# Stick-breaking attention: two heads scored in the two halves of TensorE's rows, triangular sums from two parts of the softplus

## The chip, the cores and the metric

One NeuronCore of a Trainium2 chip runs the whole program. The metric is device time in microseconds (us) from launch to end; lower is better. Three runs of the kernel before gave 775.49, 776.06 and 776.16 us, so its time is their median, 776.06 us.

## What is computed

Two transformer layers over 256 tokens of width 1024. Layer 0 mixes with stick-breaking attention (8 heads of 64) beside an S5 state-space model, layer 1 with a sparse attention; each mixer is followed by a layer norm, a mixture of 16 experts and another layer norm. The change touches the stick-breaking attention of layer 0 alone:

```python
def stick_breaking_attention(q, k, v):      # heads of 64, scale = 1/8
    for i in range(L // Q_BLOCK):           # 2 blocks of 128 queries
        z = einsum('bqhd,bkhd->bhqk', q[:, q0:kend], k[:, :kend]) * scale
        mask = s[None, :] < t[:, None]
        log_1mb = where(mask, -softplus(z), 0.0)
        after = cumsum(log_1mb, axis=3, reverse=True) - log_1mb
        w = where(mask, exp(log_sigmoid(z) + after), 0.0)
        outs.append(einsum('bhqk,bkhd->bqhd', w, v[:, :kend]))
```

With z - softplus(z) for log_sigmoid(z), the exponent is z minus the sum of the softplus from the key itself to the last allowed key.

## The kernel before

Keys lie on the partitions and queries in the free dimension, so a head's scores are one PSUM tile `z` of 384 used columns: 256 for the first 128 keys against all queries, 128 for the second 128 keys against the second 128 queries. `stick` (line 1210) returns three steps, which `mixer0` (line 1067) calls by hand as S, W and O:

- `scores(h)`, lines 1215 to 1230: two float32 matmuls with 64 rows of contraction (L1219 with 256 columns, L1220 with 128), whose operands lie in partitions 0 to 63 for even heads and 64 to 127 for odd ones; then two bfloat16 matmuls (L1222) that add -1e30 where the mask forbids. Then softplus(z) = max(z, 0) + ln(1 + exp(-|z|)): three ScalarE activations of 128x384 (L1225, L1227, L1228) and one VectorE operation (L1229), into a tile `sp` of the pool `b2` (9 slots).
- `weights(h)`, lines 1232 to 1240: three float32 matmuls with 128x128 triangles of -1 (L1234, one with 256 columns and two with 128) subtract the running sums inside PSUM; ScalarE takes the exponential (L1239).
- `values(hp)`, lines 1242 to 1252: for a pair of heads, four float32 matmuls (L1250), each head in one half of the output's partitions, and the split of the result into two float32r parts (L1251, L1252).

A float32 matmul stands in the trace as two instructions (two passes), a float32r one as one.

PSUM has two pools of four banks, `acc` and `mm`. Each `z` holds an `acc` bank from its scores until its exponential (L1239). After the heads the same four `acc` banks become `out`, the sums of the output projection: first the residual (L259, 32 instructions in this mixer), then jobs of float32r matmuls in three terms (L203 to L205 in `mm3`).

Between the heads' steps stand other steps of the mixer: `kq(j)` (L985, 32 instructions each for the keys and the queries of a pair of heads, copied out by ScalarE at L1128 and L1131), the S5 kernel (L868), the transposes of `s5_transpose` (L895 on TensorE, eight copies of 128x512 by ScalarE at L896), `s5_inputs` (L905, which needs all of these copies), the S5 states on VectorE (L920 to L931) and `s5_output` (L957 on TensorE, which needs the states), its GELU (L1060 to L1065), transposes (L973), and the gated unit behind them.

Weights come by DMA in tiles of 1 MB in the pool `u` (20 slots of 8 KB a partition), which holds the mixer's large work tiles as well. `issue` (line 131) orders further tiles as long as fewer than a cap are ahead; SyncE issues them in order and waits where the slot given to a tile is not free yet.

The order of the calls in `mixer0` is written by hand and serves as priority; a scheduler then fixes the order on each engine when the program is built, and lets a later step ahead where an earlier one isn't ready. Only in the mixture of experts is TensorE's order exactly as written.

Of the kernel before, what the change touches and what calls it, by code (L numbers as in the profile page):

```python
# [10 lines left out]
F32 = mybir.dt.float32  # L11
# [8 lines left out]
P = 128  # L20
D = 1024
KC = D // P
T = 256
# [28 lines left out]
class K:  # L52
# [47 lines left out]
    def mm(self, shape=(P, 512), dt=F32):  # L100
        return self.psp.tile(list(shape), dt, tag="mm", bufs=4, name=self.uid("mm"))
# [965 lines left out]
    def mixer0(self):  # L1067
# [79 lines left out]
        kq = lambda j: (cols(k_out(j)), cols(q_out(j)))  # L1147
        kq(0), kq(1)
        self.s5_toeplitz(self.s5_kernel(ca, vx[:, 1].rearrange("p (a r n) -> p a r n", a=16, r=2)), kts)
        S(0), S(1)  # L1150
        kq(2)
        S(2), S(3)
        kq(3)
        W(0), S(4)
        self.s5_transpose(bbp[0], w1t[0])
        W(1), S(5)
        self.s5_transpose(bbp[1], w1t[1])
        O(0), W(2)
        self.stage(10)
        ps = self.s5_inputs(U, w1t)  # L1160
        self.issue(CAP[1])
        states = self.s5_states(ps, X, bbp[1].rearrange("p a d h -> p (a d h)").rearrange("p (j n) -> p j n", j=4))
        ys = self.s5_output(U, X, kts, ca, w1t[0].rearrange("p a n -> p (a n)"))
        n = lambda g: next(g, None)
        n(states), W(3), O(1), S(6), n(states), W(4), n(states), S(7), n(states), W(5), O(2), n(states), W(6), n(states)
        W(7), O(3)
        self.table("sigmoid_and_others")
        n(ys), n(ys)
# [41 lines left out]
    def stick(self, qT, kT, V, oa):  # L1210

        nc = self.nc
        st = {}

        def scores(h):
            s = slice((h % 2) * 64, (h % 2) * 64 + 64)
            z = self.acc()
            k, q = kT[s, h // 2], qT[s, h // 2]
            nc.tensor.matmul(z[:, 0:T], k[:, 0:P], q, start=True, stop=False, skip_group_check=True)  # L1219
            nc.tensor.matmul(z[:, T:T + P], k[:, P:T], q[:, P:T], start=False, stop=False, skip_group_check=True)  # L1220
            for c in (0, T):
                nc.tensor.matmul(z[:, c:c + P], self.identb, self.negb, start=False, stop=False, skip_group_check=True)  # L1222

            sp = self.b2((P, 384))
            a = nc.scalar.activation(sp, z[:, 0:384], AF.Abs)  # L1225
            self.follow(a, self.logs)
            nc.scalar.activation(sp, sp, AF.Exp, scale=-1.0)  # L1227
            nc.scalar.activation(sp, sp, AF.Ln, bias=1.0)  # L1228
            nc.vector.scalar_tensor_tensor(sp, z[:, 0:384], 0.0, sp, ALU.max, ALU.add)  # L1229
            st[h] = (z, sp)  # L1230

        def weights(h):
            z, sp = st[h]
            mm = lambda o, l, r, stop: nc.tensor.matmul(z[:, o[0]:o[1]], l, r, start=False, stop=stop, skip_group_check=True)  # L1234
            mm((0, T), self.ntri[:, 0], sp[:, 0:T], False)
            mm((P, T), self.ntri[:, 1], sp[:, T:T + P], True)
            mm((T, T + P), self.ntri[:, 0], sp[:, T:T + P], True)
            w = self.b2((P, 384))
            nc.scalar.activation(w, z[:, 0:384], AF.Exp)  # L1239
            st[h] = w  # L1240

        def values(hp):
            o = self.mm()
            for kb in range(2):
                for c in range(2):
                    h = hp * 2 + c
                    w = st[h]
                    r = w[:, 0:T] if kb == 0 else w[:, T:T + P]
                    d = o[c * 64:c * 64 + 64, 0:T] if kb == 0 else o[c * 64:c * 64 + 64, P:T]
                    nc.tensor.matmul(d, V[:, kb, h * 64:h * 64 + 64], r, start=(kb == 0), stop=(kb == 1), skip_group_check=True)  # L1250
            nc.scalar.activation(oa[:, 0, hp], o[:, 0:T], AF.Copy)  # L1251
            nc.vector.tensor_tensor(oa[:, 1, hp], o[:, 0:T], oa[:, 0, hp].bitcast(F32), ALU.subtract)  # L1252

        return scores, weights, values


# [479 lines left out]
```

## Time and profile before

| what | value |
|---|---|
| median of three runs | 776.06 us |
| the profiled execution's own time | 776.09 us |
| its span, first to last instruction | 774.4 us |
| TensorE matmul busy | 752.6 us (97%) |
| VectorE, ScalarE, GpSimd busy | 326.3, 207.4, 46.8 us |
| bytes moved by DMA | 241.00 MB, mean 311 GB/s |

The span is the time between the first and the last instruction in the trace; 1.7 us of the execution's time lie outside it. Busy times of matmuls overlap, since a matmul's record lasts from its start to the modelled arrival of its last result. What a matmul costs in a dense stretch is the distance from its start to the start of the next.

### The profile page before, as it was taken

To read this page: it belongs to the slowest core of one execution; us is meant where nothing else is said; L and a number is where in the kernel's file an instruction comes from. 1 tells how busy PE (TensorE), PEld (TensorE's weight loads), DVE (VectorE), ACT (ScalarE), POOL (GpSimd) and SP (SyncE) were. 2 spreads that over 40 slices of the span, in tenths; PEclk is the share of its full clock that TensorE was granted. 3 is DMA by queue.
4 is the path that set the end of the run, shared out by engine and by line. 5 is a ranking of instruction groups with operands and counts; after the bars stand their busy time and mean duration, and the time that the engine had idled before them with its cause. 6 is when DMAs were issued, how large, how long until landed. Compare 5 with 4: busy or idle time off the path is not lost. (4 is left out here: it accounts for less than half of the span.)

```text
span 774.4 us, 10523 instructions
## 1 busy us (share of the span) xinstructions
PE 752.6 (97%) x4115; PEld 415.4 (54%) x4115; DVE 326.3 (42%) x836; ACT 207.4 (27%) x421; POOL 46.8 (6%) x45
## 2 busy tenths in 40 slices
PE   9999999999999999999899999999999999999993
PEld 7588778643434334333878666687434334343332
DVE  9992647611212112114956799836212112211123
ACT  1344435211101101001625577632121001011002
POOL 1010000002000000001020142300002000000000
PEclk9999999999999999999999999999999999999998
DMA  8839879889999999999975100397799999999921
GB/s 320 312 110 183 312 281 409 289 308 381 348 423 421 421 422 421 421 417 421 421 251 209 55 1 0 149 386 281 261 368 372 401 421 421 421 421 421 419 90 59
DMA packets 42540, 241.00 MB, mean 311 GB/s; under 512 B 8145, under 2 KB 9681, under 8 KB 15569
## 3 DMA queue, kind: packets, MB, share of 16 engines
q1 hardware_dynamic: 42480, 240.23, 79.8%
q8 instruction: 34, 0.56, 0.3%
q14 instruction: 26, 0.20, 0.1%
HBM read 238.38 MB, written 1.84 MB: 310 GB/s over the span
## 5 line engine op out<-in xcount | busy, mean ns | idle before, releaser
L493 PE MATMUL mm<-u,s 128*64 128x512 f32 x960 | 219.4, 598 | 0.0
L493 PEld LDWEIGHTS mm<-u,s 128*64 128x64 f32 x960 | 63.9, 136 | 120.3 <-issue 107.7
L523 PE MATMUL mm<-u,b 128*64 128x512 f32 x512 | 113.1, 593 | 0.0
L528 ACT ACTIVATE b<-mm,gslot 128x512 fp32r<-128x512 f32 x32 | 22.0, 688 | 256.1 <-PE mm L523 253.2
L529 DVE SCALAR_TENSOR_TENSOR b<-mm,gslot,b 128x512 fp32r<-128x512 f32 x32 | 24.0, 750 | 146.9 <-ACT b L528 146.9
L523 PEld LDWEIGHTS mm<-u,b 128*64 128x64 f32 x512 | 36.4, 137 | 71.9 <-issue 70.2
L195 DVE TENSOR_TENSOR s<-u,s 128x1024 fp32r<-128x1024 f32 x37 | 45.5, 1235 | 28.4 <-ACT s L192 28.3
L576 DVE TENSOR_TENSOR b<-b,mm 128x256 f32<-128x256 f32 x32 | 12.0, 418 | 106.9 <-PE mm L493 106.8
L192 ACT ACTIVATE s<-u 128x1024 fp32r<-128x1024 f32 x37 | 38.7, 1056 | 42.0 <-PE acc L205 29.0
L985 PE MATMUL mm<-u,u 128*128 128x256 f32 x208 | 48.0, 392 | 0.6 <-DMA u<-w_in 0.6
L985 PEld LDWEIGHTS mm<-u,u 128*128 128x128 f32 x208 | 40.7, 197 | 7.4 <-issue 1.7
L354 ACT ACTIVATE s<-mm,c_k_all 128x256 f32<-128x256 f32 x32 | 18.1, 565 | 96.7 <-PE mm L469 96.7
L469 PE MATMUL mm<-b,u 128*128 128x256 f32 x160 | 39.0, 325 | 0.0
L203 PE MATMUL acc<-s,u 128*128 128x512 f32 x96 | 38.0, 396 | 0.5 <-ACT u L1205 0.5
L534 PE MATMUL acc<-b,b 128*128 128x512 f32 x128 | 38.4, 421 | 0.1
L205 PE MATMUL acc<-s,u 128*128 128x512 f32 x96 | 37.8, 394 | 0.0
L204 PE MATMUL acc<-s,u 128*128 128x512 f32 x96 | 37.5, 391 | 0.0
L534 PEld LDWEIGHTS acc<-b,b 128*128 128x128 f32 x128 | 21.4, 188 | 28.4 <-issue 22.7
L469 PEld LDWEIGHTS mm<-b,u 128*128 128x128 f32 x160 | 30.0, 190 | 6.3 <-issue 4.9
L588 DVE COPY b<-mm 128x512 f32<-128x512 f32 x16 | 11.1, 692 | 45.2 <-PE mm L587 45.2
L356 DVE TENSOR_SCALAR s<-mm,c_k_all 128x256 f32<-128x256 f32 x32 | 16.8, 542 | 24.1 <-PE mm L469 23.8
L469 PE MATMUL mm<-b,s 128*128 128x256 f32 x96 | 23.5, 285 | 0.0
(309 smaller groups left out, 1002.2 us busy)
## 6 DMA issues: line engine op xcount, KB each, us to landing
u<-moe SPq DMA_DIRECT2D x180, 1024.0 KB, 11.9
u<-w_in SPq DMA_DIRECT2D x26, 1024.0 KB, 15.0
u<-w_in SPq DMA_DIRECT2D x10, 512.0 KB, 6.9
s<-moe SPq DMA_DIRECT2D x4, 1024.0 KB, 5.8
b<-moe SPq DMA_DIRECT2D x16, 256.0 KB, 8.3
u<-moe SPq DMA_DIRECT2D x8, 512.0 KB, 16.8
u<-xT SPq DMA_DIRECT2D x4, 256.0 KB, 5.7
out<-u SPq DMA_DIRECT2D x4, 256.0 KB, 4.3
```

What stands on the lines that cost most here:

```text
L192: a = self.nc.scalar.activation(s[:, 0], x, AF.Copy)
L195: self.mark = self.nc.vector.tensor_tensor(s[:, 1], x, s[:, 0].bitcast(F32), ALU.subtract)
L203: mm(o, l[0], r[0], start=first, stop=False, skip_group_check=True)
L204: mm(o, l[0], r[1], start=False, stop=False, skip_group_check=True)
L205: self.tail = mm(o, l[1], r[0], start=False, stop=last, skip_group_check=True)
L469: nc.tensor.matmul(pg[:, 0:T], x[:, t, k * P:(k + 1) * P], g.bitcast(F32) if m == 1 else g, start=(i == 0), stop=(i == 2 * m - 1))
L493: self.mark = nc.tensor.matmul(h[c * 64:(c + 1) * 64], xe[:, k, e + c], w[c], start=(k == 0), stop=(k == KC - 1))
L523: self.mark = nc.tensor.matmul(y[c * 64:(c + 1) * 64], hx[:, f, c * 64:(c + 1) * 64], w[:, c * 512:c * 512 + 512], start=(f == 0), stop=(f ...
L528: nc.scalar.activation(yh, y, AF.Copy, scale=gs)
L529: nc.vector.scalar_tensor_tensor(yl, y, gs, yh.bitcast(F32), ALU.mult, ALU.subtract)
L534: self.tail = nc.tensor.matmul(out[half][t], sT[:, t * P:(t + 1) * P], yy, start=False, stop=(p == 7 and j == 1), skip_group_check=True)
L985: self.mark = self.nc.tensor.matmul(ps, w[:, k * P:k * P + P], xT[:, k], start=(k == 0), stop=(k == KC - 1))
```

## The change

`scores` now takes a pair of heads. It takes two `acc` banks, issues the float32 matmuls of the two heads in turn (256 columns of the one, 256 of the other, 128 of the one, 128 of the other; one head's operands lie in partitions 0 to 63, the other's in 64 to 127), and then all four bfloat16 mask matmuls. The softplus of each head is copied by ScalarE to a float32r part, and VectorE computes the rest as a second float32r part; both parts of both heads lie in one new tile of the pool `u`. `weights` multiplies each triangle with both parts: six float32r matmuls (256, 256, 128, 128, 128, 128 columns) instead of three float32 ones. The triangles are copied once to float32r (`tr`). In `mixer0` the calls are placed anew: four calls of `scores` instead of eight, the last of them, for heads 6 and 7, ahead of `s5_inputs` and not among the states; W(1) and W(3) stand earlier as well.

```diff
@@ -1147,22 +1147,22 @@
         kq = lambda j: (cols(k_out(j)), cols(q_out(j)))
         kq(0), kq(1)
         self.s5_toeplitz(self.s5_kernel(ca, vx[:, 1].rearrange("p (a r n) -> p a r n", a=16, r=2)), kts)
-        S(0), S(1)
+        S(0)
         kq(2)
-        S(2), S(3)
+        S(1)
         kq(3)
-        W(0), S(4)
+        W(0), W(1), S(2)
         self.s5_transpose(bbp[0], w1t[0])
-        W(1), S(5)
+        W(2)
         self.s5_transpose(bbp[1], w1t[1])
-        O(0), W(2)
+        O(0), W(3), S(3)
         self.stage(10)
         ps = self.s5_inputs(U, w1t)
         self.issue(CAP[1])
         states = self.s5_states(ps, X, bbp[1].rearrange("p a d h -> p (a d h)").rearrange("p (j n) -> p j n", j=4))
         ys = self.s5_output(U, X, kts, ca, w1t[0].rearrange("p a n -> p (a n)"))
         n = lambda g: next(g, None)
-        n(states), W(3), O(1), S(6), n(states), W(4), n(states), S(7), n(states), W(5), O(2), n(states), W(6), n(states)
+        n(states), O(1), n(states), W(4), n(states), n(states), W(5), O(2), n(states), W(6), n(states)
         W(7), O(3)
         self.table("sigmoid_and_others")
         n(ys), n(ys)
@@ -1211,30 +1211,43 @@
 
         nc = self.nc
         st = {}
-
-        def scores(h):
-            s = slice((h % 2) * 64, (h % 2) * 64 + 64)
-            z = self.acc()
-            k, q = kT[s, h // 2], qT[s, h // 2]
-            nc.tensor.matmul(z[:, 0:T], k[:, 0:P], q, start=True, stop=False, skip_group_check=True)
-            nc.tensor.matmul(z[:, T:T + P], k[:, P:T], q[:, P:T], start=False, stop=False, skip_group_check=True)
-            for c in (0, T):
-                nc.tensor.matmul(z[:, c:c + P], self.identb, self.negb, start=False, stop=False, skip_group_check=True)
-
-            sp = self.b2((P, 384))
-            a = nc.scalar.activation(sp, z[:, 0:384], AF.Abs)
-            self.follow(a, self.logs)
-            nc.scalar.activation(sp, sp, AF.Exp, scale=-1.0)
-            nc.scalar.activation(sp, sp, AF.Ln, bias=1.0)
-            nc.vector.scalar_tensor_tensor(sp, z[:, 0:384], 0.0, sp, ALU.max, ALU.add)
-            st[h] = (z, sp)
+        tr = self.b2((P, 2, P), F32R)
+        nc.scalar.activation(tr, self.ntri, AF.Copy)
+
+        def scores(hp):
+
+            zs = [self.acc() for _ in range(2)]
+            rows = [slice(c * 64, c * 64 + 64) for c in range(2)]
+            for part in range(2):
+                for z, s in zip(zs, rows):
+                    k, q = kT[s, hp], qT[s, hp]
+                    if part == 0:
+                        nc.tensor.matmul(z[:, 0:T], k[:, 0:P], q, start=True, stop=False, skip_group_check=True)
+                    else:
+                        nc.tensor.matmul(z[:, T:T + P], k[:, P:T], q[:, P:T], start=False, stop=False, skip_group_check=True)
+            for z in zs:
+                for c in (0, T):
+                    nc.tensor.matmul(z[:, c:c + P], self.identb, self.negb, start=False, stop=False, skip_group_check=True)
+            parts = self.u([P, 2, 2, 512], F32R)
+            for c, z in enumerate(zs):
+
+                sp = self.b2((P, 384))
+                a = nc.scalar.activation(sp, z[:, 0:384], AF.Abs)
+                self.follow(a, self.logs)
+                nc.scalar.activation(sp, sp, AF.Exp, scale=-1.0)
+                nc.scalar.activation(sp, sp, AF.Ln, bias=1.0)
+                nc.vector.scalar_tensor_tensor(sp, z[:, 0:384], 0.0, sp, ALU.max, ALU.add)
+                hl = parts[:, c]
+                nc.scalar.activation(hl[:, 0, 0:384], sp, AF.Copy)
+                nc.vector.tensor_tensor(hl[:, 1, 0:384], sp, hl[:, 0, 0:384].bitcast(F32), ALU.subtract)
+                st[hp * 2 + c] = (z, hl)
 
         def weights(h):
-            z, sp = st[h]
-            mm = lambda o, l, r, stop: nc.tensor.matmul(z[:, o[0]:o[1]], l, r, start=False, stop=stop, skip_group_check=True)
-            mm((0, T), self.ntri[:, 0], sp[:, 0:T], False)
-            mm((P, T), self.ntri[:, 1], sp[:, T:T + P], True)
-            mm((T, T + P), self.ntri[:, 0], sp[:, T:T + P], True)
+            z, hl = st[h]
+            for o, l, c, n in ((0, 0, 0, T), (P, 1, T, P), (T, 0, T, P)):
+                for j in range(2):
+                    nc.tensor.matmul(z[:, o:o + n], tr[:, l], hl[:, j, c:c + n], start=False, stop=o > 0 and j == 1,
+                                     skip_group_check=True)
             w = self.b2((P, 384))
             nc.scalar.activation(w, z[:, 0:384], AF.Exp)
             st[h] = w
```

## Rows read from the trace of the kernel before

**Rows 1.** The page: TensorE's busy time; TensorE and DMA busy tenths in 40 slices.

```profile
PE 752.6 (97%) x4115; PEld 415.4 (54%) x4115; DVE 326.3 (42%) x836; ACT 207.4 (27%) x421; POOL 46.8 (6%) x45
...
PE   9999999999999999999899999999999999999993
...
DMA  8839879889999999999975100397799999999921
```

**Rows 2.** Stretches of mixer 0: us, busy per engine, granted clock, DMA share, GB/s.

```profile
52.00:70.08 18.08, 18.08 (x93) 15.23 (x89) 9.90 (x11) 8.80 (x18) 2.37 (x2) 1.00 0.70 147
70.08:83.64 13.56, 13.35 (x199) 11.72 (x197) 1.11 (x2) 8.33 (x18) 0.00 (x0) 1.00 1.15 291
83.64:99.36 15.72, 15.72 (x103) 11.74 (x99) 12.54 (x20) 7.58 (x16) 0.00 (x0) 1.00 0.78 276
99.36:118.70 19.34, 19.33 (x248) 13.92 (x248) 10.25 (x15) 7.59 (x11) 0.00 (x0) 1.00 0.76 291
```

**Rows 3.** Timeline, TensorE, scores of heads 0 and 1: start us, length us, instruction.

```profile
51.99 0.70 PE L1219 MATMUL acc<-u 64*128 64x256 f32 x2
52.52 0.38 PE L1220 MATMUL acc<-u 64*128 64x128 f32 x2
52.84 0.28 PE L1222 MATMUL acc<-c_k_bits 128*128 128x128 bf16 x2
...
54.02 0.43 PE L985 MATMUL mm<-u,u 128*128 128x256 f32 x1
```

**Rows 4.** The same timeline: masks, transposes, triangular sums, values.

```profile
72.55 0.29 PE L1222 MATMUL acc<-c_k_bits 128*128 128x128 bf16 x2
72.67 1.37 PE L895 MATMUL mm<-c_k_all,u 128*128 128x128 f32 x11
73.88 1.04 PE L1234 MATMUL acc<-b,b 128*128 128x256 f32 x6
74.75 1.15 PE L895 MATMUL mm<-c_k_all,u 128*128 128x128 f32 x9
...
77.92 0.87 PE L1250 MATMUL mm<-b,u 128*64 128x256 f32 x8
78.72 1.14 PE L1234 MATMUL acc<-b,b 128*128 128x256 f32 x6
```

**Rows 5.** The same timeline: float32r matmuls of 256 columns, then of 160 columns.

```profile
119.93 0.28 PE L203 MATMUL mm<-u,s 128*128 128x256 f32 x1
120.05 0.28 PE L204 MATMUL mm<-u,s 128*128 128x256 f32 x1
...
171.47 0.45 PE L505 MATMUL mm<-R,b 128*128 128x160 f32 x2
171.85 0.65 PE L493 MATMUL mm<-b,s 128*64 128x512 f32 x2
```

**Rows 6.** Groups, weight loads, 52 to 126 us: busy us, mean ns | idle before.

```profile
L203 PEld LDWEIGHTS mm<-u,s 128*128 128x128 f32 x16 | 3.0, 191 | 0.0
...
L1222 PEld LDWEIGHTS <-c_k_bits 128*128 128x128 bf16 x16 | 0.9, 97 | 1.0
```

**Rows 7.** Timeline, TensorE: values of heads 2 and 3 with scores of head 6.

```profile
84.72 0.65 PE L1250 MATMUL mm<-b,u 128*64 128x256 f32 x2
...
87.25 0.43 PE L1234 MATMUL acc<-b,b 128*128 128x256 f32 x1
```

**Rows 8.** Groups of ScalarE, then VectorE, from 52 us on.

```profile
L1227 ACT ACTIVATE b<-b 128x384 f32<-128x384 f32 x8 | 4.2, 521 | 0.1
...
L1229 DVE SCALAR_TENSOR_TENSOR b<-acc,b 128x384 f32<-128x384 f32 x8 | 4.4, 554 | 17.7 <-ACT b L1228 17.7
```

**Rows 9.** First expert layer: issue and landing of its last weights; their first matmul.

```profile
L144 SPq DMA_DIRECT2D u<-moe x1: 328/328/328, 331.9 to 331.9; - x1
...
DMA to landing us min/median/max: 16.2/16.2/16.2
...
360.60 1.94 PE L523 MATMUL mm<-u,b 128*64 128x512 f32 x8
```

## The prediction

> **What bounds the kernel now.** I read the page first: TensorE's matmuls are busy 97% of the span and its row of slices is full from end to end, while DMA drops in several slices [rows 1]. Matmul records overlap, so this says only that the engine seldom stands still; what a matmul costs must come from distances between starts. Then the mixer that is changed, cut into stretches at its landmarks: W(0) at 70.08 us, the end of `s5_inputs` at 83.64, the start of `s5_output` at 99.36, the gated unit at 118.70 [rows 2]. TensorE is filled in all four, VectorE is long only in the third (12.54 of 15.72 us, the S5 states), ScalarE at most 8.33 of 13.56 us. So a microsecond of matmuls saved here should end the mixer a microsecond earlier, unless a chain on another engine comes up behind it.
>
> Last, whether the rest of the program passes the gain on. In the first expert layer DMA is full [rows 1], which could swallow it. The last tile of its weights was issued at 331.9 us, landed 16.2 us later (348.1), and its first matmul began at 360.60 [rows 9]: it lay ready for 12.5 us. The layer is bound by TensorE and can start some 12 us earlier before weights are missing. I carry a gain of 5 us to the end in full.
>
> **Scores.** Heads 0 and 1 run from 51.99 to 54.02 us, 2.03 us [rows 3], between other shapes on both sides. Within a head, L1219 takes 0.53 and L1220 0.32 us: its four passes (two of 256 columns, two of 128) would be 0.65 us at the pace of L1234, which puts 1024 columns through in 0.87 us without a change of shape (73.88 to 74.75 [rows 4]), and the other 0.20 us is what it costs to go from one shape of the array to another (the first weight load isn't hidden, the last result drains). No row of before shows two row halves at work together. The nearest row is L1250: the same eight passes of 256, 256, 128 and 128 columns for two heads, halved in the output's columns and not in the rows: 77.92 to 78.72, 0.80 us [rows 4], so the halves ran side by side. The four mask matmuls behind it cost 0.06 us each (72.55 to 72.67 for two [rows 4]), 0.24 us. New pair: 1.04, and 0.05 for a weight load of 128 columns instead of 64: 1.09 us. Saved 0.94 a pair, four pairs: **3.8 us**. If the halves don't run side by side, only one entry into the shape and one way out of it are saved in each pair, some 0.3 us: 1.2 us in all. I take 3.8, since nothing in the shapes but the direction of the split differs, and keep 1.2 as the end.
>
> The Trainium skill (TensorE: Matmul & The Clock Gate, Part 3: Packing small matmuls) says that packed matmuls start and end strictly in program order; if a float32 matmul's two passes stand together in that order, the second head's first pass could only start with the first head's second. By that rule a pair takes about one pass of 256 columns more, 0.2 us, and the sum below would be 4.2 instead of 5.0 us. The 0.80 us of L1250 leaves no room for such a lag between column halves; for row halves no row shows it.
>
> **Triangular sums.** The three float32 matmuls cost the 0.87 us just read, eight times. The new six are float32r. With 256 columns one costs 0.12 us (119.93 to 120.05 [rows 5]). With 128 columns none is in the trace, so bounds: below, the masks' 0.06 us in bfloat16; in the middle 0.11 us, the pace of the transposes L895, one pass of 128 columns with a weight load each (eleven in 72.67 to 73.88 [rows 4]); above, 0.22 us, if 128 columns in float32r cost as much as the two float32 passes. The pair with 160 columns, 0.38 us with the way in and out of the shape (0.2), is near 0.1 each [rows 5], which excludes little but the upper end. Weight loads decide: a float32r load of 128 columns lasts 191 ns, the bfloat16 one 97 [rows 6], so I expect the load to set the pace, 0.11 us. Head: 2 x 0.12 + 4 x 0.11 = 0.68, saved 0.19, eight heads **1.5 us**. Ends: 2 x 0.12 + 4 x 0.06 = 0.48, saved 3.1; 2 x 0.12 + 4 x 0.22 = 1.12, lost 2.0.
>
> The Trainium skill (the same page, Weight-path perf modes) gives fast weight loads to all types but FP32. If float32r counts as another type, this case goes to its lower end, and the sum would be 6.6 us. The 191 ns speak against it.
>
> **Moved calls.** S(6) ran between the halves of O(1), with a change of shape each time: 84.72 to 87.25, 2.53 us [rows 7], where O(1) by itself costs 0.80 and a head's scores 1.02 (half of 2.03). With S(3) before `s5_inputs` this weaving goes: 0.7 less one entry of 0.2, **0.5 us** (0 to 0.7, as the scheduler may weave something else in).
>
> **Added work beside TensorE.** Eight copies of 128x384 on ScalarE, at about the 0.52 us of L1227 [rows 8]: 4.2 us. Eight subtractions on VectorE at about the 0.55 us of L1229 [rows 8]: 4.4 us. Heads 0 to 3 have their softplus long before W(0), with both engines half idle from 52 to 70 us [rows 2]; the copy of the triangles lies before that. In the second stretch it gets narrow. ScalarE had 8.33 us there. Heads 6 and 7 come in with 3 x 0.52 each, four copies, and W(3)'s exponential: 8.3 + 3.1 + 2.1 + 0.5 = 14.0 us. TensorE's work of that stretch becomes 13.6 + 1.1 (W(3)) + 2.0 (S(3)) less 1.9 (two pairs) and 0.8 (four W): 14.0 us. What is queued behind ScalarE's copies are the copies L896 for which `s5_inputs` waits; but the softplus of heads 6 and 7 can finish behind them. In the third stretch TensorE sinks from 15.7 to about 11 us (W(3), S(6) and S(7) gone, four cheaper W), and VectorE's states, 12.5 less two softplus operations, become as long. The cover is there: the 48 matmuls L203 to L205 of the first output jobs, 512 columns and so twice 0.12 us each [rows 5], can run before `s5_output`. I take **0.8 us** of new waits, between 0 and 3.
>
> **Slots.** Each pair's two parts take a 1 MB slot of `u` until both its W are done, two or three at a time from 55 to 93 us. They come from those of the weights ahead. At the program's mean of 311 GB/s a tile is 3.4 us of DMA, three are 10. SyncE issues in order, so the S5 kernel's own transfers queue behind a weight tile that waits for a slot; `s5_output` at 99.36 us waits for them. DMA has room to catch up before 107 us (shares 0.70 to 0.78 in three of the four stretches [rows 2]), and 12.5 us of cover stand at the far end [rows 9], so I cost this at nothing; without that cover each missing tile costs its 3.4 us.
>
> **Sum.** 3.8 + 1.5 + 0.5 - 0.8 = 5.0 us off the profiled execution's 776.09: 771.1 us. The median of the runs is 776.06, the same within 0.03.
>
> **The rivals.**
> - *The row halves run one after the other, or lag.* Scores save 1.2 instead of 3.8: 773.7 us; with the lag 771.9. For it: no row shows row halves together. Against it: column halves do.
> - *Float32r weights load fast.* The triangles save 3.1: 769.5 us. Against it: 191 ns.
> - *Another engine takes TensorE's place.* ScalarE is as full as TensorE in the second stretch, VectorE in the third; if each makes TensorE wait some 2 us, about 1 us is left: 775 us. For it: both sums above are even. Against it: much of that work isn't needed until later, and TensorE has other matmuls to run.
> - *Slower: the parts of heads 4 to 7 wait for slots.* If the scheduler gives freed slots to weights first, W(4) to W(7) come late, and meanwhile their `z` tiles hold all four `acc` banks, so that neither the residual nor the output jobs can run. Then only O(1) and `s5_output` are left to TensorE (19.3 us of the fourth stretch less 47 output matmuls at 0.24 and 8 transposes at 0.11: 7.2 us), and from there each us of delay is a us lost: it needs more than about 7 us of delay to eat the 5 us and the cover. Ten to fifteen us give 779. Against it: the calls of `scores` stand ahead of the weights in the hand-written order.
>
> **How the numbers follow.** Forecast 0.50 (by itself 769.9 to 772.8), halves in turn or lagging 0.18, fast loads 0.12, another engine 0.12, slots or something unseen that is slower 0.08. A difference of 0.2%, 1.55 us, is about what a measurement of this kernel can tell from no change. The first three are faster by more; the fourth is mostly within it: faster 0.80, same 0.11, slower 0.09. The range goes from 768.8 (fast loads and no waits) to 775.5 (half of the fourth case); below and above it lies some 0.17.
>
> **What would show it.** A pair's eight passes in about 0.85 us with two starts close together, not 1.4 us; the six triangle matmuls of a head with about 0.11 us between starts of 128 columns; `s5_inputs` ending near 82 us instead of 83.64, with W(3) and the last scores ahead of it; `s5_output` with no idle time before it; the first matmul on the first expert layer's last weights at 355.6 instead of 360.60 us. It is wrong if a gain in the mixer is seen and given back in the experts (weights), or if TensorE stands idle between 70 and 100 us on ScalarE or VectorE.

## The result, and the profile after

| what | before | after |
|---|---|---|
| median of four runs each | 775.78 us | 786.15 us |
| ratio, 95% interval | | 1.0133 (1.012 to 1.0145) |
| span of the profiled execution | 774.4 us | 784.6 us |
| first scores of layer 0 (TensorE) | 51.99 us | 51.56 us |
| first expert matmul of layer 0 (L493) | 151.36 us | 158.02 us |
| first expert matmul of layer 1 (L493) | 544.51 us | 554.93 us |
| TensorE's end | 764.33 us | 774.84 us |

The change makes the kernel 10.4 us slower. The forecast was 771.1 us, faster, with a range up to 775.5.

The work ahead of the first scores begins and ends some tenths of a us earlier or later from one profile to the next. So two distances, read from the profiled execution of each kernel, are used from here on: **A**, from the first scores to the first expert matmul of layer 0 (the changed mixer and the norm behind it), and **B**, from there to the first expert matmul of layer 1 (nothing in it is edited). Before has A 99.37 and B 393.15 us, after has A 106.46 and B 396.91 us: 7.1 us are lost in the mixer, and 3.8 us in code that the change doesn't touch. From the last of these marks to TensorE's end both take 219.8 to 219.9 us.

The page of after: TensorE's busy line, TensorE's slices and, in tenths of full speed, the clock that TensorE was granted in each (a slice is 19.6 us).

```profile
PE 750.6 (96%) x4115; PEld 414.8 (53%) x4115; DVE 331.2 (42%) x844; ACT 210.6 (27%) x430; POOL 47.0 (6%) x45
...
PE   8999599999999999999899999999999999999994
...
PEclk9999799999999999999999998999999999999998
```

Against [rows 1], one slice has sunk by more than a tenth, the fifth (78 to 98 us): TensorE is busy half of it, and its granted clock is down too. A second dip of the clock, in the 25th slice (around 480 us), has no dip of TensorE's busy time over it. Stretches of the mixer around the first one (us; busy us of PE, PEld, DVE, ACT, POOL; granted clock, DMA share, GB/s):

```profile
70.00:84.50 14.50, 13.90 (x211) 12.09 (x209) 3.19 (x6) 12.07 (x28) 0.00 (x0) 1.00 0.91 210
84.50:94.19 9.69, 0.05 (x2) 0.01 (x1) 9.45 (x15) 0.04 (x1) 0.00 (x0) 0.61 0.67 222
94.19:110.00 15.81, 15.81 (x230) 10.68 (x230) 4.95 (x11) 5.25 (x9) 0.00 (x0) 0.81 0.48 196
```

From 84.5 to 94.19 us TensorE and ScalarE do next to nothing and VectorE is busy 9.45 of the 9.69 us; in [rows 2] TensorE was filled in the same place. TensorE's timeline names the wait (in brackets: idle us before, and what ended it):

```profile
84.04 0.50 PE L1249 MATMUL acc<-u,b 128*128 128x256 f32 x2
94.19 2.40 PE L1249 MATMUL acc<-u,b 128*128 128x256 f32 x10 [9.64 <-DVE u L1242]
```

L1249 are the triangular sums. Two of the twelve matmuls of heads 4 and 5 run at 84.04, by their 256 columns the ones that need only the high parts; the other ten need or follow a low part, which VectorE computes at L1242. VectorE's timeline, with the softplus of heads 6 and 7 (L1239), the first and the last of the S5 states, and the low parts of heads 4 and 5:

```profile
81.64 1.02 DVE L1239 SCALAR_TENSOR_TENSOR b<-acc,b 128x384 f32<-128x384 f32 x2 [7.48 <-ACT b L1238]
83.36 0.69 DVE L920 TENSOR_TENSOR u<-mm,u 128x512 f32<-128x512 f32 x1 [0.70 <-PE mm L905]
...
92.99 0.67 DVE L922 TENSOR_TENSOR u<-u 128x496 f32<-128x496 f32 x1
93.58 1.02 DVE L1242 TENSOR_TENSOR u<-b,u 128x384 fp32r<-128x384 f32 x2
```

And ScalarE's, with the high parts of heads 4 and 5 (first row) and of heads 6 and 7:

```profile
81.91 0.93 ACT L1241 ACTIVATE u<-b 128x384 fp32r<-128x384 f32 x2
...
83.00 0.94 ACT L1241 ACTIVATE u<-b 128x384 fp32r<-128x384 f32 x2
```

The softplus of heads 4 and 5 was done by 74.2 us (their L1239 ran at 73.13 for 1.02), its copy stands on ScalarE behind the whole softplus of heads 6 and 7, and its subtraction, possible from 82.8 us, stands on VectorE behind fourteen operations of the states. Each engine works its list in the order fixed when the program is built; none of these copies and subtractions waits for its data when its turn comes.

### The profile page after: what moved, and what is told of

Its sections match the earlier page's. It is cut to its first block, busy times and chain, and to the rows that moved or that the text cites. A ratio compares the mean times of both kernels' runs of the same rounds, so it can differ in the third digit from the quotient of the medians.

```text
span 784.6 us, 10534 instructions
## 1 busy us (share of the span) xinstructions
PE 750.6 (96%) x4115; PEld 414.8 (53%) x4115; DVE 331.2 (42%) x844; ACT 210.6 (27%) x430; POOL 47.0 (6%) x45
## 5 line engine op out<-in xcount | busy, mean ns | idle before, releaser
L493 PE MATMUL mm<-u,s 128*64 128x512 f32 x960 | 219.4, 598 | 0.0
L493 PEld LDWEIGHTS mm<-u,s 128*64 128x64 f32 x960 | 63.8, 136 | 120.3 <-issue 107.8
L985 PE MATMUL mm<-u,u 128*128 128x256 f32 x208 | 46.4, 381 | 2.2 <-DMA u<-w_in 2.0
L985 PEld LDWEIGHTS mm<-u,u 128*128 128x128 f32 x208 | 39.0, 190 | 8.9 <-issue 2.1
```

The costliest lines, as they stand in the source:

```text
L493: self.mark = nc.tensor.matmul(h[c * 64:(c + 1) * 64], xe[:, k, e + c], w[c], start=(k == 0), stop=(k == KC - 1))
L985: self.mark = self.nc.tensor.matmul(ps, w[:, k * P:k * P + P], xT[:, k], start=(k == 0), stop=(k == KC - 1))
```

## The experiments

Undoing the change in steps gave kernels whose profiles can be laid side by side. The times of before beside these runs were 775.6 to 776.2 us. A and B belong to one profiled execution, the time is the median of all runs; where the two differ much, the text says so.

| kernel | A, us | B, us | time, us | ratio to before |
|---|---|---|---|---|
| before | 99.37 | 393.15 | 775.6 to 776.2 | |
| moved calls alone | 97.77 | 393.84 | 775.29 | 1.0006 (0.9989 to 1.0022) |
| + row pairs, float32 sums | 95.65 | 393.88 | 773.19 | 0.9972 (0.9958 to 0.9986) |
| + split sums, states put behind them | 95.16 | 395.51 | 772.43 | 0.9954 (0.9937 to 0.997) |
| the change (split sums, states ahead) | 106.46 | 396.91 | 786.15 | 1.0133 (1.012 to 1.0145) |
| split sums alone, old calls and scores | 109.58 | 393.86 | 788.13 | 1.0167 (1.0138 to 1.0197) |

### The states behind the low parts

```diff
-        half(x0, ps, (C, S), 0, 1, ALU.add, (t0, t1))
+        self.follow(v.tensor_tensor(t0, ps[0], C, ALU.mult), self.low)
+        v.tensor_tensor(t1, ps[1], S, ALU.mult)
+        v.tensor_tensor(x0, t0, t1, ALU.add)
...
-                nc.vector.tensor_tensor(hl[:, 1, 0:384], sp, ...)
+                self.low = nc.vector.tensor_tensor(hl[:, 1, 0:384], sp, ...)
```

> Edit: the first of the recurrence's state operations on VectorE is put after the last subtraction of a low part; places and calls are those of the change. Theory A (only VectorE's order does the harm): the states begin some 1 to 2 us later than in the change, head 4's sums start near 85 us in place of 94.2 us, the granted clock stays at full, and the time is 772 to 776 us. Rival (states are what the end waits for, and setting them back costs as much as is won): head 4's sums come early, but TensorE then idles 5 us or more before the recurrence's outputs, and the time is 780 us or more.

772.43 us, 13.7 us less than the change, with the same work; 11.3 us of it are in A. (The profiled execution took 773.68 us, the others 772.2 to 772.5.) VectorE's timeline: the low parts (now L1244) stand ahead of nearly all of the states.

```profile
84.08 1.02 DVE L1244 TENSOR_TENSOR u<-b,u 128x384 fp32r<-128x384 f32 x2
...
85.34 1.02 DVE L1244 TENSOR_TENSOR u<-b,u 128x384 fp32r<-128x384 f32 x2
```

TensorE's timeline: the sums of heads 4 and 5 (now L1251) run through, and the only wait over 1 us ahead of the gated unit is one for the states, later.

```profile
84.03 2.00 PE L1251 MATMUL acc<-u,b 128*128 128x256 f32 x12
...
94.73 0.45 PE L959 MATMUL mm<-u,u 64*32 64x128 f32 x16 [1.05 <-DVE u L922]
```

So the order on VectorE alone makes the hole, and setting the states back by up to 3 us costs about 1 us. The rival falls.

### The low parts on GpSimd

```diff
-                nc.vector.tensor_tensor(hl[:, 1, 0:384], sp, ...)
+                (nc.gpsimd if hp > 1 else nc.vector).tensor_tensor(hl[:, 1, 0:384], sp, ...)
```

> Edit: the subtractions that make the low parts of heads 4 to 7 run on GpSimd, all else is the change. The tiles are handed out as in the change, only VectorE's queue is left out of the path. Theory A (VectorE's queue is what delays the low parts; their high parts are there from 81.9 us): the low parts follow at 83 to 85 us, TensorE waits for head 4's sums under 3 us, the time is 772 to 776 us. Rival (the tile itself comes free late on the chip): the subtractions wait on GpSimd as they did on VectorE, the idle time stays at 8 us or more, and the time is 784 to 787 us.

Its median is 783.38 us, but the profiled execution took 777.27. The other four took 783.1 to 783.7 us at a mean granted clock of 0.983 to 0.984 against 0.993; none of them has a profile, so where they lose these 6 us more is not shown. Rows of TensorE's timeline:

```profile
83.77 1.58 PE L1249 MATMUL acc<-u,b 128*128 128x256 f32 x12
...
94.39 0.63 PE L957 MATMUL mm<-u,u 128*32 128x128 f32 x2 [4.84 <-DVE u L1265]
```

Head 4's sums start at 83.77 us without a wait: the place of the parts was free on the chip and the data was there, only VectorE's list was in the way. Then, after a wait of 1.24 us for the states, the next thing in the same list stops TensorE for 4.84 us: L1265, the low part of the attention's outputs, which stands behind the states as well. The expectation of 772 to 776 us missed this second victim of one cause, and the slower four runs.

### Two tiles set aside early

```diff
+        room = [self.u([P, 2, 2, 512], F32R) for _ in range(2)]
...
-            parts = self.u([P, 2, 2, 512], F32R)
+            parts = room[hp % 2]
```

> Edit: the two tiles that hold the parts of heads are set aside once, before the first scores, and the four head pairs use them in turn; the work and the order of the calls are those of the change. Theory A (place: the parts of heads 4 to 7 get a tile late in the build's plan, so their subtractions stand behind the recurrence's states L920 to L922 in VectorE's queue, and TensorE idles 9.64 us before head 4's sums, and then works about 3 us longer at a lower granted clock): the subtractions come before the states, the idle time before head 4's sums falls under 2 us, and the time is 771 to 774 us. Theory B (the order comes from the order of the calls, wherever the parts lie): the idle time stays near 9.6 us and the time near 786 us. Theory C (the change costs time elsewhere too, the sums or the moved calls): the idle time goes, yet the time stays above 778 us.

Only the place of the parts differs from the change. ScalarE now copies heads 4 and 5 at 74.17 us, right behind their softplus, and not at 81.91:

```profile
74.17 0.94 ACT L1242 ACTIVATE u<-b 128x384 fp32r<-128x384 f32 x2
```

VectorE's low parts (L1243) of the four heads:

```profile
74.73 1.03 DVE L1243 TENSOR_TENSOR u<-b,u 128x384 fp32r<-128x384 f32 x2 [0.29 <-ACT u L1242]
...
82.61 0.56 DVE L1243 TENSOR_TENSOR u<-b,u 128x384 fp32r<-128x384 f32 x1 [0.95 <-ACT u L1242]
...
85.11 0.55 DVE L1243 TENSOR_TENSOR u<-b,u 128x384 fp32r<-128x384 f32 x1
```

No wait over 0.6 us is left on TensorE up to the gated unit, and A is 96.34 us, 10.1 less than in the change. So the order of the lists came from the place of the parts: a tile taken anew for each pair gets its slot of `u` so late in the build's reckoning that the states go ahead. (That the reckoning sets it so is argued from this run; no trace shows the reckoning.) The time, 776.11 us (ratio 1.0, 0.9983 to 1.0018), is above the 771 to 774 expected, because B gave back most of what A won against before: 395.47 us, 2.3 more than before's, with a wait of 0.99 us (below) and the granted clock at 0.89 in a stretch of layer 1.

```profile
385.00:400.00 15.00, 15.00 (x72) 11.67 (x73) 8.18 (x15) 5.78 (x6) 1.43 (x3) 0.89 0.62 224
```

Its ten runs spread from 773.0 to 778.8 us, and their mean granted clock with them, from 0.997 to 0.990.

### The three parts of the change alone

The moved calls, with before's scores and sums:

```diff
-        W(0), S(4)
+        W(0), W(1), S(4), S(5)
...
-        n(states), W(3), O(1), S(6), n(states), W(4), n(states), S(7), n(states), W(5), ...
+        n(states), O(1), n(states), W(4), n(states), n(states), W(5), ...
```

> Edit: the kernel before, with its scores head by head and its float32 sums, in the changed kernel's order of calls. Theory A (the moved calls are worth the 0.5 us of the prediction and make no hole of their own): the first expert matmul of layer one comes 0 to 1 us earlier than before's 151.4 us, and the time is 775 to 776.5 us, against about 776.2 us. Rival (the calls in this order make TensorE wait for VectorE, whatever stands in them): idle time of 3 us or more ahead of head 4's sums, and 779 us or more.

775.29 us, not to be told from before; A is 1.60 us shorter, more than the 0 to 1 expected. Row pairs with before's sums (the change without `parts` and `tr`):

```diff
-                st[hp * 2 + c] = (z, hl)
+                st[hp * 2 + c] = (z, sp)
...
-            for o, l, c, n in ((0, 0, 0, T), (P, 1, T, P), (T, 0, T, P)):
...
+            mm((0, T), self.ntri[:, 0], sp[:, 0:T], False)
+            mm((P, T), self.ntri[:, 1], sp[:, T:T + P], True)
+            mm((T, T + P), self.ntri[:, 0], sp[:, T:T + P], True)
```

> Edit: scores in two halves of TensorE's rows and the order of the calls as in the change, but the triangular sums are the three float32 matmuls of before, from one softplus, with no parts, no copies and no subtractions. Theory A (the harm is the parts' alone): no idle time over 2 us before head 4's sums, each head's sums take 0.87 us again, and the time is the before kernel's less the scores' 3.8 us and up to 1 us for the calls: 771 to 773 us. Rival (the moved calls alone make the hole): idle time of 5 us or more stands before head 4's sums, and the time is 780 us or more.

773.19 us, just above the range expected, A another 2.12 us shorter, no wait over 0.3 us on TensorE up to the gated unit. And the split sums in before's calls, with scores head by head:

```diff
+            if h % 2 == 0:
+                st["u"] = self.u([P, 2, 2, 512], F32R)
+            hl = st["u"][:, h % 2]
+            nc.scalar.activation(hl[:, 0, 0:384], sp, AF.Copy)
+            nc.vector.tensor_tensor(hl[:, 1, 0:384], sp, hl[:, 0, 0:384].bitcast(F32), ALU.subtract)
-            st[h] = (z, sp)
+            st[h] = (z, hl)
...
```

> Edit: the kernel before, with its scores head by head and its order of calls; only the sums are taken from the two parts of the softplus. Theory A (the parts are late wherever their subtractions stand behind the states L920 to L922 on VectorE; with one head of scores at a time heads 6 and 7 are subtracted among the states, so the waits are short): the sums take 0.68 us a head in place of 0.87, the waits give most of it back, and the time is 774.5 to 777 us. Rival (the parts alone make the hole, whatever the calls): idle time of 5 us or more, and 780 us or more.

788.13 us: here theory A fell and the rival held. TensorE's row, and the row of VectorE that it waits for, behind the last of the states (L922, ending at 95.46):

```profile
95.98 2.40 PE L1243 MATMUL acc<-u,b 128*128 128x256 f32 x10 [5.82 <-DVE u L1236]
```

```profile
95.38 1.02 DVE L1236 TENSOR_TENSOR u<-b,u 128x384 fp32r<-128x384 f32 x2
```

The hole belongs to the parts, whatever the calls. (A is 3.1 us longer here than in the change, though this wait is shorter; where the rest is lost was not followed.)

### What the hole costs beside its own length

Twenty-one matmuls on constants were put ahead of head 4's sums, then ten (`FILL`):

```diff
+        for i in range(FILL):
+            m = self.nc.tensor.matmul(pt, self.c512[:, 0:P], self.c512, start=True, stop=True, skip_group_check=True)
...
-        n(states), O(1), n(states), W(4), ...
+        n(states), O(1), n(states), self.fill(), W(4), ...
```

> Edit: the changed kernel with 21 matmuls of 128x512 float32 on constants (0.43 us apart where the kernel issues such ones, 9.0 us in all) put between head pair 1's outputs and head 4's sums, where TensorE idles 9.64 us; their result is read by nobody. Theory A (the idle time costs twice: 9.64 us itself, and some 3 us because the granted clock is at half until about 100.4 us): the granted clock stays at 1.00 in 94 to 110 us, the first expert matmul of layer one comes at 154.5 to 155.5 us in place of 158.0 us, and the time is 782 to 784 us. Rival (the clock costs nothing there, since VectorE's states end last anyway): that matmul stays at 157.5 to 158.5 us and the time at 786 us.

Twenty-one were too many: a float32 matmul is two passes, so they took 18.26 us in place of 9.0, and the sums began at 104.88 us; 792.75 us, not the 782 to 784 of theory A. With ten:

> Edit: as the run with the filled hole, but 10 float32 matmuls of 128x512 in place of 21; that run's took 18.26 us (0.87 us each), so that ten take 8.7 us and fit into the idle 9.64 us. Theory A (the granted clock's fall after the hole costs 2 to 3 us in layer one): the clock stays at 1.00 from 84.5 to 110 us, head 4's sums start at 94 to 95.5 us, and their distance to the first expert matmul is 61 to 62 us in place of 63.8 us. Rival (the fall costs nothing in layer one, the longer filler only gave VectorE time to get ahead): that distance stays at 63.3 us or more.

785.1 us. TensorE's rows, with the sums at L1260:

```profile
85.98 10.52 PE L312 MATMUL mm<-c_k_all 128*128 128x512 f32 x20 [2.14 <-DVE u L931]
95.94 1.88 PE L1260 MATMUL acc<-u,b 128*128 128x256 f32 x12
```

Its stretches, the clock ahead of the sums and from them on:

```profile
84.50:95.94 11.44, 9.96 (x21) 4.32 (x21) 11.23 (x18) 0.00 (x0) 0.00 (x0) 0.85 0.66 236
95.94:110.00 14.06, 14.05 (x235) 8.82 (x234) 3.12 (x7) 5.24 (x9) 0.00 (x0) 1.00 0.44 178
```

From the start of head 4's sums to the first expert matmul it is 61.86 and 61.85 us in these two and 63.83 in the change, where two of their twelve matmuls were done ahead of the hole: with the clock at 1.00 (2.4 GHz) behind the hole 1.98 us are saved. In the change itself no wait over 0.3 us stands behind the hole up to the gated unit, so VectorE's head start in the filled runs doesn't explain them. The hole costs its 9.64 us, and 2.0 us more for the work behind it at a granted clock of 0.81. So theory A holds, though not as written for the run with ten: its matmuls had to wait 2.14 us themselves, and the clock fell then and came back ahead of the sums. There the saving is eaten by sums that begin 2.0 us later, counted from the first scores, and A is 106.48 us.

### The loss in layer 1

VectorE's timeline in before, in the sparse attention of layer 1: two scalings of probabilities (L1506), then the low part of the query (L1381), for which TensorE waits 0.23 us; and GpSimd's product (L1503) beside them.

```profile
467.85 0.47 DVE L1506 TENSOR_SCALAR u<-u,sm 128x128 f32<-128x128 f32 x2
468.35 1.28 DVE L1381 TENSOR_TENSOR u<-mm,u 64x512 fp32r<-64x512 f32 x2
```

```profile
468.10 1.13 POOL L1503 TENSOR_TENSOR b<-b,sm 128x512 f32<-128x512 f32 x1 [2.38 <-ACT u L1380]
```

The same in after, where they are L1519, L1394 and L1516:

```profile
474.54 1.23 DVE L1519 TENSOR_SCALAR u<-u,sm 128x128 f32<-128x128 f32 x2
475.80 1.28 DVE L1394 TENSOR_TENSOR u<-mm,u 64x512 fp32r<-64x512 f32 x2
```

```profile
474.45 1.04 POOL L1516 TENSOR_TENSOR b<-b,sm 128x512 f32<-128x512 f32 x1 [2.05 <-DVE sm L1512]
```

The lists are the same; what differs is who came first. In before VectorE's scalings began 0.25 us ahead of GpSimd's product and took 0.47 us; in after the product began 0.09 us ahead of them, and they took 1.23. TensorE then waits 1.00 us for L1394, and the granted clock falls; TensorE's row and the stretches behind it:

```profile
476.54 0.39 PE L1501 MATMUL acc<-u,u 128*128 128x256 f32 x1 [1.00 <-DVE u L1394]
```

```profile
478.00:480.00 2.00, 2.00 (x12) 0.93 (x8) 1.94 (x6) 0.86 (x4) 0.00 (x0) 0.80 0.00 0
480.00:486.00 6.00, 6.00 (x30) 3.61 (x31) 4.64 (x13) 3.25 (x13) 1.59 (x2) 0.50 0.00 0
486.00:488.00 2.00, 2.00 (x19) 1.34 (x15) 1.14 (x6) 0.61 (x3) 0.49 (x1) 1.00 0.00 0
```

The Trainium skill (SBUF — State Buffer, Who interferes with whom) says that a VectorE instruction in a two-port mode, which `tensor_scalar` can enter, contends with GpSimd for a shared pair of ports, and that whoever issues first gets the pair for the whole instruction while the other is blocked. The rows agree: 0.47 us or 1.23 us for the same two scalings, the difference, 0.76 us, being most of the product's 1.04.

To test it, the change, with its hole, but with the two scalings called behind the query's low part:

```diff
-                    v.tensor_scalar(x[:, b], ...)
+                    f = lambda x=x, b=b, t=t: v.tensor_scalar(x[:, b], ...)
+                    if h == HELD:
+                        hd.setdefault("held", []).append(f)
+                    else:
+                        f()
...
         q_turn(1)
+        [f() for f in hd["held"]]
```

> Edit: the changed kernel, its hole in layer one left as it is; in layer two the two scalings of one head's probabilities on VectorE (L1519), which run 1.0 us while a GpSimd product runs beside them, are put behind the subtractions of the query's low part (L1394) that TensorE waits for. Theory A (the 3.74 us that layer two loses come from that wait: 0.77 us longer than before, and after it the granted clock is at half for some 7 us, worth 3 us): the wait at 476.5 us falls under 0.3 us, the clock stays at 1.00 there, the stretch from the second layer's first L203 of attention to its first expert matmul takes 148.1 us again and the time is 782 to 783.5 us. Rival (the clock falls in layer two for another reason, for instance as an aftermath of layer one): the stretch stays above 150 us and the time at 785 us or more.

783.13 us, 3.0 less than the change. The wait at L1394 is gone and the clock stays at 1.00:

```profile
474.00:486.00 12.00, 11.12 (x76) 6.59 (x77) 11.16 (x32) 9.02 (x31) 3.13 (x3) 1.00 0.00 1
```

A wait of 0.88 us appears elsewhere, so B is 393.61 us and not before's 393.15. In the run with row pairs alone TensorE stood idle for the same 1.00 us at the same place and the clock stayed at 1.00 (the wait, and one of the stretches behind it):

```profile
465.64 0.38 PE L1495 MATMUL acc<-u,u 128*128 128x256 f32 x1 [1.00 <-DVE u L1388]
```

```profile
470.00:472.00 2.00, 2.00 (x20) 1.50 (x21) 2.00 (x6) 1.53 (x8) 0.18 (x1) 1.00 0.00 0
```

Its B was 393.88 us. So of B's 3.8 us 0.7 is the wait and 3.0 the clock. The wait alone doesn't bring the clock down: eight profiles have it (0.99 to 1.02 us, the change's and those of seven runs), and in the seven runs the clock stayed at 1.00 behind it. The hole of layer 0, which this run keeps, isn't enough either. What the fall needs beside the wait is not settled.

### Both orders mended, and the banks

> Edit: the changed kernel with both orders mended: the states follow the last subtraction of a low part (as in the run that put the states behind), and layer two's two scalings follow the query's low parts. Theory A (the change's own gain is some 4.6 us in layer one; layer two then gives nothing back): the first expert matmul of layer one at 146.5 to 147 us, the stretch from layer two's first L203 of attention to its first expert matmul at 148.1 us, the time 771 to 772.5 us against 775.6 to 776.2 us of before. Rival (layer two's stretch stays at 148.8 us or more, since something else decides its order, or the granted clock falls there): 772.5 us or more.

772.03 us, ratio 0.9948 (0.9934 to 0.9961), inside theory A's range; A is 95.17 us, as in the run with the states behind. The profiled execution, at 773.97 us the longest of the five (the others 771.7 to 772.2), went as the rival said: B was 395.20 us, the clock falling elsewhere (0.83 in 380 to 390 us). The same order of layer 1 with row pairs and float32 sums:

> Edit: row pairs and moved calls with before's float32 sums, and layer two's two scalings put behind the query's low parts. It stands beside the run with both orders mended and tells what the split sums are worth by themselves. Theory A (the sums' 0.19 us a head, 1.5 us in all, is mostly given back in waits for the parts): within 0.8 us of that run, 771.5 to 773 us. Rival (the split sums are worth their 1.5 us): 1 us or more slower than that run.

772.95 us, 0.9 us more than with the split sums, which lies between the 0.8 of theory A and the 1 of the rival. A, free of what happens in layer 1, is 95.67 us: the split sums by themselves are worth 0.5 us of it, and not 1.5. One thing was still short of the forecast, the scores. In the change the third pair of heads goes one head behind the other (TensorE's timeline):

```profile
69.17 0.70 PE L1225 MATMUL acc<-u 64*128 64x256 f32 x2
69.70 0.38 PE L1227 MATMUL acc<-u 64*128 64x128 f32 x2
69.82 0.70 PE L1225 MATMUL acc<-u 64*128 64x256 f32 x2
70.36 0.38 PE L1227 MATMUL acc<-u 64*128 64x128 f32 x2
70.67 0.40 PE L1230 MATMUL acc<-c_k_bits 128*128 128x128 bf16 x4
70.90 0.28 PE L895 MATMUL mm<-c_k_all,u 128*128 128x128 f32 x1
```

69.17 to 70.90 is 1.73 us; the fourth pair takes 1.82. Right ahead of them stand the sums that free their two `acc` banks. A bank is free when the exponential has read it (L1252 on ScalarE; the second bank of the third pair, then of the fourth):

```profile
69.28 0.49 ACT L1252 ACTIVATE b<-acc 128x384 f32<-128x384 f32 x1 [0.19 <-PE acc L1249]
...
77.78 0.49 ACT L1252 ACTIVATE b<-acc 128x384 f32<-128x384 f32 x1
```

These end at 69.77 and 78.27 us, and the second head's scores begin at 69.82 and 78.33. So in the last run, which has both orders mended, the sums were called earlier as well:

```diff
         S(1)
+        W(0), W(1)
         kq(3)
-        W(0), W(1), S(2)
+        S(2)
+        W(2), W(3)
...
-        O(0), W(3), S(3)
+        O(0), S(3)
```

> Edit: the run with both orders mended, and in layer one the sums of heads 0 and 1 are called ahead of the last columns of keys and queries, those of heads 2 and 3 ahead of the S5 transposes, so that both accumulator banks of head pairs 2 and 3 are free when their scores begin. Theory A (the third and fourth pair took 1.73 and 1.82 us instead of 1.09 because their two banks come free one after the other, behind the sums of two heads just ahead, and the plan then puts one head behind the other): all four pairs take about 1.09 us, some 1.4 us are saved in layer one, the first expert matmul comes at 145.2 to 146 us and the time is 770.3 to 771.3 us. Rival (the two heads are put one behind the other for another reason, or the sums called early wait for their parts): pairs 2 and 3 stay at 1.7 us or TensorE waits over 1 us before a sum, and the time is 771.7 us or more.

771.04 us, ratio 0.9941 (0.9928 to 0.9955), the best of all, A 94.11 us. TensorE's timeline, the second and third pair and the sums behind the third:

```profile
59.95 0.70 PE L1231 MATMUL acc<-u 64*128 64x256 f32 x4
...
61.01 1.79 PE L1255 MATMUL acc<-u,b 128*128 128x256 f32 x12
...
69.69 0.70 PE L1231 MATMUL acc<-u 64*128 64x256 f32 x4
...
70.75 1.56 PE L1255 MATMUL acc<-u,b 128*128 128x256 f32 x12
72.15 1.93 PE L898 MATMUL mm<-c_k_all,u 128*128 128x128 f32 x16
```

Both pairs take 1.06 us, and all four run side by side (the first 1.09, the fourth 1.19). A gains 1.1 us, a little less than the 1.4 expected.

## Why the prediction was wrong

**The step that failed** is "added work beside TensorE", with "slots". The prediction summed each engine's busy time by stretch, found room, and took 0.8 us of new waits and nothing for slots. Busy time was the wrong measure. VectorE had room for eight subtractions of 0.5 us; what it had no room for was two of them behind 10.3 us of states (83.36 to 93.66). The question it never asked of the eight subtractions is where each stands in VectorE's list, and who waits meanwhile. It asked it for ScalarE's copies alone: the softplus of heads 6 and 7 did go behind the copies L896, as it said, but the build put the copies of heads 4 and 5 behind that softplus too.

**The rival that came true** was named, with its place: parts of heads 4 to 7 late, W(4) to W(7) late, banks held, nothing left for TensorE, "779 us", at a chance of 0.08. Its mechanism was off. No slot was waited for on the chip: with GpSimd doing the subtraction, the same tiles were written and the sums started at 83.77 us. As far as the runs tell, the slot acted in the build, where it settled the order of ScalarE's and VectorE's lists: two tiles set aside early took 10.1 us off A. "The calls of `scores` stand ahead of the weights in the hand-written order" was no argument, since the order of the calls is a wish that the scheduler overrules for a step it holds to be not ready.

**What was missing from its price.** The hole was 9.64 us, just under the ten to fifteen assumed; the 779 us counted on work of the fourth stretch to hide some 7 us of delay, but TensorE is busy for 0.05 of the 9.69 us. A is 11.3 us above that of the run with the states behind, 9.64 + 2.0 less 0.3. The 2.0 us of clock behind the hole and the 3.8 us of layer 1 were in no term. The prediction took code that isn't edited as passing a gain on unchanged. It does so for DMA, as it said: from the first expert matmul of layer 0 to the transposes of the norm behind its experts (L345) it is 217.8 us in before, in the change and in the last run, and from layer 1's experts to the end nothing changed by more than 0.1 us. In layer 1's attention it doesn't, where a shift of some 0.3 us between two engines decides over 0.7 us, and a clock over 3.0.

**Scores: 3.8 us forecast.** The price of a pair was right: 51.56 to 52.65 us, 1.09 us. The two heads' first passes start together, and so do the second ones; two narrow windows of TensorE's timeline of after show two instructions each with one start:

```profile
51.56 0.49 PE L1225 MATMUL acc<-u 64*128 64x256 f32 x2
```

```profile
51.88 0.38 PE L1225 MATMUL acc<-u 64*128 64x256 f32 x2
```

So halves of the rows work side by side as those of the columns did. The lag that the prediction read out of the Trainium skill (TensorE: Matmul & The Clock Gate, Part 3: Packing small matmuls) doesn't come about: starts stay in order, but the two heads' passes alternate. The count was wrong: two pairs saved 0.94 us, the others 0.30 and 0.21 (2.03 less 1.73 and 1.82), 2.4 us in all; the step from the moved calls to row pairs alone measured 2.1 of A. (The 2.03 us, taken from heads 0 and 1, were also a little high for the others: heads 4 and 5 cost 0.97 each in before, 71.70 to 72.67 and 76.08 to 77.05.) A pair needs two banks at once, and the prediction spoke of the four held banks only in its rival. With the banks freed early 1.1 us more of A came.

**Triangular sums: 1.5 us forecast, 0.5 got.** The size was right. With work of the same shape behind them two heads take 1.40 us (70.75 to 72.15 in the last run), 0.70 a head where 0.68 was forecast and 0.87 was before [rows 4]. Of 0.17 x 8 = 1.4 us some 0.9 is given back. The run with the states behind has two waits that the run without the split doesn't have: 0.60 us ahead of L895 for ScalarE, which is at the softplus of heads 4 and 5 when TensorE gets there, and 1.05 us for the states. Together they are more than the 0.9; TensorE's order differs between these two runs as well, so the account doesn't close to the tenth. The fast weight load of the other rival is refuted: 0.70 and not 0.48 a head. The Trainium skill's rule for it (TensorE: Matmul & The Clock Gate, Weight-path perf modes) leaves out FP32; by the pace, float32r doesn't get it either.

**Moved calls: 0.5 us less 0.8 of waits forecast.** By themselves they gave 1.6 us of A and no new wait over 0.3 us. That term was too low.

**What would show it**, point by point: starts together, yes; 0.11 us between starts of 128 columns, yes for three of a head's four (one is 0.06; 0.70 a head in all); `s5_inputs` ending near 82 us, no (83.26, with more work ahead of it, as two pairs were not side by side); "TensorE stands idle between 70 and 100 us on ScalarE or VectorE", the sign that it is wrong, was what came. `s5_output` had no idle time right before it, but behind the hole that says little; and the first matmul on the first expert layer's last weights came at 367.27 us, not at 355.6 (355.17 in the last run). With the order mended and the banks freed the sum does come out: A shrinks by 5.3 us where 5.0 were forecast, and the time is 771.04 us. That is partly luck: the row pairs gave 3.2 us (2.1 and 1.1) of 3.8, the sums 0.5 of 1.5, and the moved calls 1.6 where they were to cost 0.3 with the new waits; and the last run has layer 1's order changed too.

## What to carry to other kernels

In this kernel a small operation added to a half idle engine was free only where it stood ahead of the engine's next long run in its list: look for the longest uninterrupted run on each engine that gets work (10.3 us of states here), ask what happens to TensorE if the new operation lands behind it, and pin the order if the answer is bad (one added dependency was worth 11.3 us of A, and 13.7 of the time). Where a scheduler fixes the order at build time, a new tile seems able to change the order even if its slot is free on the chip. And an edit that makes two things run side by side needs the resources of both at the same moment.

## What the runs showed of the hardware

- Idle time of TensorE can cost more than its length: after 9.64 us idle the granted clock was 0.61 over the hole and 0.81 over the next 15.8 us, worth 2.0 us; after 1.00 us idle in layer 1 it was 0.50 (1.2 GHz) for 6 us, worth 3.0 us, in one kernel and not in seven others. The filled hole shows the same: behind a wait of 2.14 us the clock fell in the run with ten matmuls, behind 2.13 us it stayed at 1.00 in the run with twenty-one. Three profiles (two tiles set aside, states behind, both orders mended) show such a fall between 380 and 400 us as well (0.89 over 15 us in the first; in the second B is 1.6 us longer for it). Differences of 1 to 3 us here need not come from the edit.
- Two scalings on VectorE take 0.47 us or 1.23 us, by whether they begin just ahead of or just behind a product on GpSimd.
- Two heads' scores in the two halves of the rows cost 1.06 to 1.19 us where one after the other cost 1.94 to 2.03.
